# Turning the first half of x block by block in the prologue of a one-core fp32 decoder step

## The chip, the cores and the metric

The kernel runs on one core of one Trainium2 chip. The metric is the device time of one execution in microseconds; the time before is the median of three runs. The profile shows one execution. TensorE appears as two rows: PE (matmuls) and PEld (loads of the stationary operand); DVE is VectorE, ACT is ScalarE, POOL is GpSimd, SP is SyncE, which issues nearly all DMAs.

## What is computed

One layer of a hybrid decoder over 1024 new tokens and 8 x 8 decode tokens, width 1024: a half-step SwiGLU FFN (`ffn1`), token mixing (a pooling branch and a Mamba-2 SSD branch), a second half-step FFN, a final RMSNorm. The change touches only the start, which prepares and begins the first FFN:

```python
def rmsnorm(x, g):
    y = xf * lax.rsqrt(jnp.mean(xf * xf, axis=-1, keepdims=True) + EPS)
    return (y * g.astype(jnp.float32)).astype(x.dtype)

def swiglu(x, w_in, w_out):
    gu = x @ w_in
    g, u = gu[..., :D_FF], gu[..., D_FF:]
    return (jax.nn.silu(g) * u) @ w_out
...
x = x + 0.5 * swiglu(rmsnorm(x, norm_ffn1[l]), ffn1_w_in[l], ffn1_w_out[l])
```

## The kernel before, in words

Everything is fp32. A product is made of three fp32r products: each operand is split into a high part (`hi`, `wh`: the value rounded to fp32r) and a low part (`lo`, `wl`: the value minus its high part), and TensorE computes wh·hi, wh·lo and wl·hi (`products`, `mm` at L176). Tokens are handled in two halves: half 0 has 512 prompt tokens, half 1 has 512 prompt tokens and the 64 decode tokens.

`load_x(h, out)` prepares one half. It loads x in blocks of 128 tokens, each as two tiles `xin` of 128 x 512 (L905, on SyncE's queue). For each block ACT squares both tiles and sums along the row (L912) into the columns of `ss`. When all blocks of the half are squared, DVE adds the two sums and scales them (L915, L916), GpSimd raises to the power -0.5 (`rsqrt`, L378), and DVE multiplies the identity by each block's factor (L922), which gives diagonal matrices `dg`. TensorE then turns and normalizes x at once: for each of the eight 128-channel groups k, four matmuls of an `xin` block against its diagonal fill one PSUM bank `ptx` (tag "ps", of which there are 8 - N_PDF = 2 banks; the other six have tag "pd"). ACT copies the bank times the RMSNorm gain to `xn` (L935), DVE rounds the same bank to `hi` (L936), and DVE (even k) or GpSimd (odd k) subtracts to get `lo` (L941). ACT and DVE do not read one bank at the same time. For half 0 `hi` and `lo` lie side by side in one tile `hl`. Half 1 has a ninth group of small matmuls `pxs` for the decode tokens.

The order of work is written as generators ("chains"). A chain is due at a value of `pe[0]`, the kernel's own running count of TensorE time, to which `mm` adds the columns / 2400 us (four times that where the moving operand is not fp32r); `tick()` after each group of matmuls steps the chains that are due, and `finish` runs one to its end. The tile framework then orders each engine's instructions by this trace order, priorities and readiness in its own schedule, and puts in all waits. So an engine's queue is fixed before the run, and an instruction waits in it for the one ahead.

At the start, `load_x` for half 0 is stepped five times (loads, then the four blocks' squares), the first four weight tiles of ffn1 are loaded and split (`load_w`, L305 to L309, kept in `ahead`; ACT makes `wh` at L308, DVE `wl` at L309; three buffers each), and `load_x` for half 1 is stepped once; it continues X1_AT = 4.0 later. The loads that must not go first are held back by `hold`: a 1x1 copy by GpSimd (L283) into the tile from something that is known late, here half 0's `ss`. Then `ffn` calls `operands`: for each half it finishes `load_x`, starts `combine` as a chain due T_AT = 2.0 later, and runs the half's plain blocks: `ffn_in_plain` computes a 128-row block of the gate and up products in two "pd" banks `pg` and `pu`, three blocks for half 0 and two for half 1. `combine` makes the sums of x that the remaining blocks, which use a Winograd scheme (matmuls `pw`), need: GpSimd subtracts (`sub`, L521), ACT and DVE split the results into tiles `X` (`put`, L529 and L530).

Of the kernel before, what the change touches and what calls it, by code (L numbers as in the profile page):

```python
# [52 lines left out]
F_Y = 0.5  # L53
X1_AT = 4.0
T_AT, T_PACE = 2.0, 1.5
TURN_AT, CONST_AT = 60.0, 40.0
HP, HP_ST, HP_EV, HP_SC = 40, 0, 60, 80
SETS = (((0,), (1,), (2,), (3,)), ((0, 1), (2,), (3,)))
# [16 lines left out]
def tile_hybrid_pool_ssd_macaron(  # L75
# [45 lines left out]
    def fx(dt=F32, name="x"):  # L121
        if stage["name"] == "mix":
            return act((P, 576), dt, name)
        return stage["p"].tile([P, 592], dt, tag="fx", bufs=N_FX, name=nm(name))

    def psum(tag="ps", name="ps"):
        npd = stage["npd"]
        return stage["ps"].tile([P, 512], F32, tag=tag, bufs=npd if tag == "pd" else 8 - npd, name=nm(name))
# [18 lines left out]
    def start(gen, delay=0.0):  # L147
        c = Chain(gen, delay)
        chains.append(c)
        return c  # L150
# [24 lines left out]
    def mm(out, lhsT, rhs, start=True, stop=True, free=False):  # L175
        T.matmul(out, lhsT, rhs, start=start, stop=stop, skip_group_check=free)  # L176
        pe[0] += max(out.free_size(), 64) / 2400.0 * (1 if rhs.dtype == F32R else 4)
# [59 lines left out]
    Abc = cp.tile([P, NH], F32, tag="Abc", name="Abc")  # L237
    Dcol = cp.tile([P, 16], F32, tag="Dcol", name="Dcol")
    hp = [0]
    late = []  # L240

    def load_consts():

# [38 lines left out]

        G.tensor_copy(t[:1, :1], src)  # L283

    def load_w(w, k0, nk, c0, ncol=P, behind=None, keep=False):

        if (k0, c0) in ahead:
            return ahead.pop((k0, c0))
        if (w.tensor.name, k0, c0) in parted:
            nth[0] += 1  # L290
            out = []
            for t, src in zip(("wh", "wl"), parted[w.tensor.name, k0, c0]):
                if nth[0] % 2:
                    o = sp.tile([P, 4 * P], F32, tag="wraw", bufs=N_RAW, name=nm(t)).bitcast(F32R)
                else:
                    o = sp.tile([P, 4 * P], F32R, tag=t, bufs=N_W, name=nm(t))
                o = o[:, : nk * P]
                dma(o.bitcast(F32), src)
                out.append(o.rearrange("p (k c) -> p k c", c=ncol))
            return tuple(out)  # L300
        raw, wh, wl = (sp.tile([P, 4 * P], d, tag=t, bufs=n, name=nm(t))[:, : nk * ncol]
                       for t, d, n in (("wraw", F32, N_RAW), ("wh", F32R, N_W), ("wl", F32R, N_W)))
        if behind is not None:
            hold(raw, behind)
        dma(raw.rearrange("p (k c) -> p k c", c=ncol),  # L305
            w[k0 * P : (k0 + nk) * P, c0 : c0 + ncol].rearrange("(k p) c -> p k c", p=P))
        with tc.high_priority(hp[0]):
            S.activation(wh, raw, AF.Copy)  # L308
            V.tensor_tensor(wl, raw, wh.bitcast(F32), op=ALU.subtract)  # L309
        if keep:  # L310
            to = [dp.tile([P, nk * P], F32, tag=nm("part"), name=nm("part")) for _ in range(2)]
            for a, b in zip(to, (wh, wl)):
                dma(a, b.bitcast(F32))
            parted[w.tensor.name, k0, c0] = to
        return wh.rearrange("p (k c) -> p k c", c=ncol), wl.rearrange("p (k c) -> p k c", c=ncol)
# [190 lines left out]
                after(p, i, banks[i])  # L506
                tick()

    def combine(h, xn, hi, lo, hl, X, pace):

        n = NPAIR[h]
        f, s_ = slice(0, n), slice(n, 2 * n)
        for p, i0, cs in (("1", 0, f), ("2", 4, f), ("3", 4, s_)):
            X[p] = [(hi[i0 + i][:, cs], lo[i0 + i][:, cs]) if h else hl[i0 + i][:, :, cs] for i in range(4)]
        for p in "6574":
            X[p] = []

        def sub(out, a, b):  # L520
            G.tensor_tensor(out, a, b, op=ALU.subtract)  # L521

        def put(src, p, a=None, b=None):
            both = None
            if a is None:
                t = act((P, 576), F32R, "X")
                a, b = t[:, f], t[:, s_]
                both = t[:, : 2 * n].rearrange("p (a b) -> p a b", a=2)
            S.activation(a, src, AF.Copy)  # L529
            V.tensor_tensor(b, src, a.bitcast(F32), op=ALU.subtract)  # L530
            X[p].append((a, b) if h else both)

        for i in range(4):
            a, b = xn[i], xn[4 + i]
            sub(a[:, s_], a[:, s_], a[:, f])
            t2 = fx(name="t2")[:, f]
            sub(t2, b[:, s_], a[:, s_])
            put(t2, "6")
            put(a[:, s_], "5")
            yield pace  # L540
            sub(a[:, f], t2, a[:, f])
            sub(b[:, f], b[:, f], t2)
            put(a[:, f], "7")
            yield pace
        yield None
        for i in range(4):
            put(xn[4 + i][:, f], "4", hi[i][:, s_], lo[i][:, s_])
            if h == 0:
                X["4"][i] = hl[i][:, :, s_]
            yield pace  # L550
# [150 lines left out]
        yield SUM_PACE  # L701
        dma(*late_.pop(0))

    def operands(prep, plain):

        X, behind = [{}, {}], []
        for h in HALVES:
            finish(prep[h][0])
            x = prep[h][1][0]
            gen = combine(h, x[3], x[1], x[2], x[4], X[h], T_PACE)  # L710

            def first(gen):
                for p in gen:
                    if p is None:
                        return
                    yield p

            c = start(first(gen), T_AT)
            plain(x[:3])
            behind.append(start(rest(c, gen)))  # L720
        for c in behind:
            finish(c)
        return X

    def ffn(wi, wo, prep, after, half=None, side=None):

        def plain(x):
            for ff in range(N_PLAIN[x[0]]):  # L730
                ffn_in_plain(wi, ff, x)

        X = operands(prep, plain)
        if side:
            side = start(side, PART_AT)
        for ff in range(N_PLAIN[1], N_PLAIN[0]):
            ffn_in(wi, ff, [(1, X[1])])
        for ff in range(N_PLAIN[0], NFF - N_APART):
            ffn_in(wi, ff, [(h, X[h]) for h in HALVES])
        for h in HALVES:  # L740
            for ff in range(NFF - N_APART, NFF):
                ffn_in(wi, ff, [(h, X[h])])
        if side:
            finish(side)
        second(wo, after, half)
# [143 lines left out]
    def load_x(h, out):  # L889
# [16 lines left out]
                raws[-1].append(t)  # L906
        late.append(ss)
        yield X1_AT if h else 0.2
        for i, (_, c0, c) in enumerate(blocks):
            for q in range(2):  # L910
                junk = act((P, 512), name="junk")
                S.activation(junk[:c], raws[i][q][:c], AF.Square, accum_out=ss[:c, q, i : i + 1])  # L912
            yield 0.5
# [6 lines left out]
        dg = [dg[:, i * P : i * P + b[2]] for i, b in enumerate(blocks)]  # L920
        for i, (_, c0, c) in enumerate(blocks):
            V.tensor_scalar_mul(dg[i][:c, :c], ident[:c, :c], ss[:c, 2, i : i + 1])  # L922
        if h == 1:
            pq = psum("ps", "pxs")
            for k in range(KD):
                mm(pq[:, k * NS : (k + 1) * NS], raws[4][k // 4][:NS, (k % 4) * P : (k % 4 + 1) * P], dg[4][:NS, :NS])
        hi, lo, xn, hl = [None] * KD, [None] * KD, [None] * KD, [None] * KD
        for k in range(KD):
            pt = psum("ps", "ptx")
            for i in range(4):  # L930
                mm(pt[:, i * P : (i + 1) * P], raws[i][k // 4][:, (k % 4) * P : (k % 4 + 1) * P], dg[i])
            x = fx(name="xn") if k >= 4 else act((P, 576), name="xn")
            a, b, both = (act((P, 576), F32R, "hi"), act((P, 576), F32R, "lo"), None) if h else pair(576)
            g = cols[:, i_g1 + k : i_g1 + k + 1]
            S.activation(x[:, :512], pt, AF.Copy, scale=g)  # L935
            V.tensor_scalar_mul(a[:, :512], pt, g)  # L936
            if h == 1:
                ps_ = pq[:, k * NS : (k + 1) * NS]
                S.activation(x[:, 512:N], ps_, AF.Copy, scale=g)
                V.tensor_scalar_mul(a[:, 512:N], ps_, g)  # L940
            (G if k % 2 else V).tensor_tensor(b[:, :N], x[:, :N], a[:, :N].bitcast(F32), op=ALU.subtract)  # L941
            hi[k], lo[k], xn[k], hl[k] = a, b, x, both
            yield 0.9
        out.append((h, hi, lo, xn, hl))
# [410 lines left out]
    st = open_stage("ffn1", N_PDF)  # L1355
    finish(start(load_cols(0, nr0)))
    prep1 = [(start(load_x(h, o)), o) for h, o in ((0, []), (1, []))]
    for _ in range(5):
        prep1[0][0].step()
    for kb in (0, 4):  # L1360
        for c0 in (0, FF):
            ahead[kb, c0] = load_w(wi1, kb, 4, c0, behind=late[0][:1, 0, :1] if kb else None)
    prep1[1][0].step()

    def turn():
# [10 lines left out]
        yield from part(ffn2_w_in[0], [(kb, 4, c0 + ff * P) for ff in range(N_PLAIN[0]) for kb in (0, 4) for c0 in (0, FF)])  # L1376
        yield from part(w_o[0], [(kb, 4, m * P) for m in range(KD) for kb in (0, 4)])

    ffn(wi1, ffn1_w_out[0], prep1, after1, side=side())
    ahead_d = in_proj(prep1m)  # L1380
    st.close()

# [587 lines left out]
```

## Time and profile before

| | before |
|---|---|
| median of 3 runs | 2871.04 us (2869.55 to 2874.98) |
| the profiled execution | 2877.41 us, span 2875.6 us |
| mean granted TensorE clock | 0.989 |
| busy, share of the span | PE 97%, PEld 91%, DVE 65%, POOL 48%, ACT 47% |
| instructions | 54690 |

Times in the profile count from the start of the span. A line such as L912 is the kernel line that issued the instruction; all matmuls of the kernel have L176 and are told apart by the tile that they write. In a row of the timeline the first number is the start, the second the length, and the square brackets give how long the engine had been idle and what ended that. One matmul of full fp32 operands, such as `ptx`, shows as two instructions.

### The profile page before, as it was taken

To read this page: it belongs to the slowest core of one execution; us is meant where nothing else is said; L and a number is where in the kernel's file an instruction comes from. 1 tells how busy PE (TensorE), PEld (TensorE's weight loads), DVE (VectorE), ACT (ScalarE), POOL (GpSimd) and SP (SyncE) were. 2 spreads that over 40 slices of the span, in tenths; PEclk is the share of its full clock that TensorE was granted. 3 is DMA by queue.
4 is the path that set the end of the run, shared out by engine and by line. 5 is a ranking of instruction groups with operands and counts; after the bars stand their busy time and mean duration, and the time that the engine had idled before them with its cause. 6 is when DMAs were issued, how large, how long until landed. Compare 5 with 4: busy or idle time off the path is not lost.

```text
span 2875.6 us, 54690 instructions
## 1 busy us (share of the span) xinstructions
PE 2775.5 (97%) x19834; PEld 2606.6 (91%) x19834; DVE 1879.0 (65%) x2912; ACT 1364.5 (47%) x3024; POOL 1378.5 (48%) x1406
## 2 busy tenths in 40 slices
PE   7999999999999999999989999899999999999998
PEld 5999999899889999999988887678999999998997
DVE  6665565777884586867765767776665554457675
ACT  5444444643454565554554446556233434445433
POOL 6566566543442355554622332332235766664522
PEclk9999999999999999999999999999999999999999
DMA  4565554787745455544377788887775332337865
GB/s 132 180 209 193 175 161 151 248 295 250 238 130 161 154 167 168 180 155 137 100 234 231 213 251 268 261 272 216 235 242 176 107 99 94 99 114 257 286 202 183
DMA packets 533488, 548.02 MB, mean 191 GB/s; under 512 B 42836, under 2 KB 373704, under 8 KB 533208
## 3 DMA queue, kind: packets, MB, share of 16 engines
q1 hardware_dynamic: 533200, 544.51, 59.5%
q8 instruction: 156, 2.56, 0.4%
q14 instruction: 116, 0.95, 0.1%
q10 hardware_dynamic: 16, 0.00, 0.0%
HBM read 391.82 MB, written 152.78 MB: 189 GB/s over the span
## 4 chain that ended last, share of the span: by engine, by line
PE 75%; DMA 7%; DVE 6%; issue 4%; POOL 4%; ACT 2%; SPq 1%; POOLq 0%; ACTq 0%; DVEq 0%
PE pw L176 43%; PE po L176 10%; PE pso L176 5%; PE pg L176 3%; PE pbp L176 3%; PE pwo L176 3%; PE pu L176 2%; DMA hr<-xq 1%; PE pgm L176 1%; DMA hp<-xq 1%; PE pyd L176 1%; PE pst L176 1%; DVE hr L781 1%; DVE wl L459 1%; POOL s L676 1%
## 5 line engine op out<-in xcount | busy, mean ns | idle before, releaser
L176 PE MATMUL pw<-X,wh 128*128 128x288 f32 (+2 forms) x2832 | 627.5, 310 | 5.0 <-ACT t L604 2.7
L176 PEld LDWEIGHTS pw<-X,wh 128*128 128x128 f32 x2832 | 462.1, 189 | 27.3 <-ACT t L604 3.2
L176 PE MATMUL pw<-X,wl 128*128 128x288 f32 (+1 forms) x1644 | 473.6, 288 | 0.8 <-DVE wl L459 0.8
L459 DVE TENSOR_TENSOR wl<-s,wh 128x512 fp32r<-128x512 f32 x288 | 245.2, 853 | 247.1 <-ACT wh L458 232.4
L176 PE MATMUL pw<-hl,wh 128*128 128x256 f32 (+1 forms) x1536 | 391.7, 328 | 3.6 <-ACT t L580 2.3
L452 POOL TENSOR_TENSOR s<-wraw,wraw 128x512 f32<-128x512 f32 x144 | 198.9, 1381 | 332.8 <-DVE wl L459 210.3
L176 PE MATMUL pw<-hi,wh 128*128 128x288 f32 x1120 | 331.7, 296 | 2.6 <-DVE t L616 1.9
L176 PE MATMUL pw<-hi,wl 128*128 128x288 f32 x1120 | 329.8, 294 | 0.0
L176 PE MATMUL pw<-lo,wh 128*128 128x288 f32 x1120 | 329.6, 294 | 0.0
L176 PEld LDWEIGHTS pw<-X,wl 128*128 128x128 f32 x1644 | 311.7, 190 | 1.0 <-DVE wl L459 1.0
L176 PE MATMUL pw<-hl,wl 128*128 128x256 f32 x1072 | 300.6, 280 | 0.9 <-DVE wl L459 0.9
L176 PEld LDWEIGHTS pw<-hl,wh 128*128 128x128 f32 x1536 | 258.8, 189 | 24.9 <-ACT t L580 2.9
L759 POOL TENSOR_TENSOR ws<-wraw,wraw 128x512 f32<-128x512 f32 x120 | 179.8, 1507 | 200.9 <-DMA wraw<-in_ffn_w_out_dram 88.5
L459 DVE TENSOR_TENSOR wl<-wraw,wh 128x512 fp32r<-128x512 f32 x216 | 185.3, 858 | 124.2 <-ACT wh L458 118.9
L458 ACT ACTIVATE wh<-s 128x512 fp32r<-128x512 f32 x288 | 181.2, 630 | 136.2 <-PE pw L176 110.0
L176 PEld LDWEIGHTS pw<-hi,wh 128*128 128x128 f32 x1120 | 210.5, 188 | 9.5 <-DVE t L616 2.5
L176 PEld LDWEIGHTS pw<-lo,wh 128*128 128x128 f32 x1120 | 210.6, 188 | 0.0
L176 PEld LDWEIGHTS pw<-hi,wl 128*128 128x128 f32 x1120 | 210.1, 188 | 0.0
L458 ACT ACTIVATE wh<-wraw 128x512 fp32r<-128x512 f32 x216 | 135.8, 629 | 151.4 <-PE pw L176 130.7
L176 PEld LDWEIGHTS pw<-hl,wl 128*128 128x128 f32 x1072 | 202.9, 189 | 1.9 <-DVE wl L459 1.9
L176 PE MATMUL po<-hh,wh 128*128 128x272 f32 x848 | 179.9, 294 | 10.1 <-ACT wh L767 8.7
L176 PE MATMUL po<-hr,wh 128*128 128x272 f32 x848 | 178.1, 291 | 3.8 <-DVE hr L781 3.8
(403 smaller groups left out, 6773.3 us busy)
## 6 DMA issues: line engine op xcount, KB each, us to landing
wraw<-in_ffn_w_out_dram SPq DMA_DIRECT2D x240, 256.0 KB
wraw<-in_ffn_w_in_dram SPq DMA_DIRECT2D x188, 256.0 KB
wraw<-in_w_in_dram SPq DMA_DIRECT2D x144, 256.0 KB
wh<-part SPq DMA_DIRECT2D x116, 256.0 KB
wl<-part SPq DMA_DIRECT2D x116, 256.0 KB
hr<-xq SPq DMA_DIRECT2D x106, 272.0 KB
xq<-s SPq DMA_DIRECT2D x66, 272.0 KB
xq<-g SPq DMA_DIRECT2D x62, 272.0 KB
```

What stands on the lines that cost most here:

```text
L176: T.matmul(out, lhsT, rhs, start=start, stop=stop, skip_group_check=free)
L452: G.tensor_tensor(t, a, b, op=op)
L458: S.activation(wh, a, AF.Copy)
L459: V.tensor_tensor(wl, a, wh.bitcast(F32), op=ALU.subtract)
L676: G.tensor_tensor(out[:, a], x0[:, a], y[:, b0], op=op)
L759: G.tensor_tensor(s, raws[0], raws[1], op=ALU.subtract if p in MINUS2 else ALU.add)
L781: V.tensor_tensor(t[:, :n].bitcast(F32R), t[:, :n], a[:, :n].bitcast(F32), op=ALU.subtract)
```

## The change

Half 0 no longer waits for its last block. Eight PSUM banks (six of tag "pd", two of "ps") are taken for the eight groups at once. As each block's squares are done, its own factor is computed (add, scale, power, diagonal for one column), and its eight matmuls fill its quarter of all eight banks. When the fourth block is done, the banks are emptied by `leave_x`, which both halves share. In it, for half 0, the `hi` of odd groups is rounded by ACT instead of DVE, and all `lo` parts are made by DVE. Half 1 is turned as before, bank by bank.

The first weight tile is loaded and split ahead of the squares in the trace; the other three tiles' splits are pinned behind everything that was traced before on their engines, and the ACT copy and the DVE rounding of half 0's group 4 are pinned behind these splits. GpSimd's subtractions in `combine` for half 0 are queued behind a 1x1 copy that waits for the fourth `lo` part, and that chain falls due at T_AT1 = 9.0 instead of T_AT = 2.0. The second half's first step, the chain of constants and that of turning x again are started when `pe[0]` already holds half 0's transposes.

```diff
+T_AT1 = 9.0
...
         with tc.high_priority(hp[0]):
-            S.activation(wh, raw, AF.Copy)
-            V.tensor_tensor(wl, raw, wh.bitcast(F32), op=ALU.subtract)
+            pin(S.activation(wh, raw, AF.Copy))
+            pin(V.tensor_tensor(wl, raw, wh.bitcast(F32), op=ALU.subtract))
...
+        if gate is not None:
+            gate = G.tensor_copy(gate, lo[3][:1, :1].bitcast(F32)).ins
+
         def sub(out, a, b):
-            G.tensor_tensor(out, a, b, op=ALU.subtract)
+            if gate is None:
+                G.tensor_tensor(out, a, b, op=ALU.subtract)
+                return
+            with tc.issue_after(gate):
+                G.tensor_tensor(out, a, b, op=ALU.subtract)
...
-            c = start(first(gen), T_AT)
+            c = start(first(gen), T_AT if h or gate is None else T_AT1)
...
         yield X1_AT if h else 0.2
+        if h == 0:
+            pts = [psum("pd" if k < 6 else "ps", "ptx") for k in range(KD)]
+            for i in range(4):
+                cut = slice(i, i + 1)
+                for q in range(2):
+                    junk = act((P, 512), name="junk")
+                    S.activation(junk, raws[i][q], AF.Square, accum_out=ss[:, q, cut])
+                V.tensor_tensor(ss[:, 2, cut], ss[:, 0, cut], ss[:, 1, cut], op=ALU.add)
+                V.tensor_scalar(ss[:, 2, cut], ss[:, 2, cut], 1.0 / D, EPS, op0=ALU.mult, op1=ALU.add)
+                rsqrt(ss[:, 3, cut], ss[:, 2, cut])
+                dg = act((P, P), name="dg")
+                V.tensor_scalar_mul(dg, ident, ss[:, 3, cut])
+                for k in range(KD):
+                    mm(pts[k][:, i * P : (i + 1) * P], raws[i][k // 4][:, (k % 4) * P : (k % 4 + 1) * P], dg)
+                yield 0.5
+            yield from leave_x(h, out, pts, None)
+            return
...
+    def leave_x(h, out, pts, pq):
+        N = NTOK[h]
+        def pin_w4(ins):
+            for w in pinned:
+                if w.ins.engine == ins.ins.engine:
+                    tc.add_manual_dep(ins.ins, w.ins.name, mybir.DependencyInfo(
+                        mybir.DependencyClass.NoSync, mybir.DependencyReason.DATA), reason="keep_in_program_order")
+            return ins
...
         for k in range(KD):
+            pt = pts(k) if h else pts[k]
...
-            S.activation(x[:, :512], pt, AF.Copy, scale=g)
-            V.tensor_scalar_mul(a[:, :512], pt, g)
+            pin = (lambda i: i) if h or k != 4 else pin_w4
+            pin(S.activation(x[:, :512], pt, AF.Copy, scale=g))
+            if h == 0 and k % 2:
+                S.activation(a[:, :512], pt, AF.Copy, scale=g)
+            else:
+                pin(V.tensor_scalar_mul(a[:, :512], pt, g))
...
-            (G if k % 2 else V).tensor_tensor(b[:, :N], x[:, :N], a[:, :N].bitcast(F32), op=ALU.subtract)
+            (G if k % 2 and h else V).tensor_tensor(b[:, :N], x[:, :N], a[:, :N].bitcast(F32), op=ALU.subtract)
...
-    for _ in range(5):
+    prep1[0][0].step()
+    first_w = load_w(wi1, 0, 4, 0)
+    for _ in range(4):
         prep1[0][0].step()
+    ahead[0, 0] = first_w
     for kb in (0, 4):
-        for c0 in (0, FF):
-            ahead[kb, c0] = load_w(wi1, kb, 4, c0, behind=late[0][:1, 0, :1] if kb else None)
+        for c0 in (FF,) if kb == 0 else (0, FF):
+            ahead[kb, c0] = load_w(wi1, kb, 4, c0, behind=late[0][:1, 0, :1] if kb else None,
+                                pin=lambda i: pinned.append(tc.keep_in_program_order(i)))
     prep1[1][0].step()
...
-    ffn(wi1, ffn1_w_out[0], prep1, after1, side=side())
+    ffn(wi1, ffn1_w_out[0], prep1, after1, side=side(), gate=late[0][:1, 3, 4:5])
```

More of the change, by code (lines that the diff above doesn't have):

```diff
@@ L239, in tile_hybrid_pool_ssd_macaron @@
     hp = [0]
-    late = []
+    late, pinned = [], []
     def load_consts():
@@ L283, in hold, with load_w @@
         G.tensor_copy(t[:1, :1], src)
-    def load_w(w, k0, nk, c0, ncol=P, behind=None, keep=False):
+    def load_w(w, k0, nk, c0, ncol=P, behind=None, keep=False, pin=lambda i: i):
         if (k0, c0) in ahead:
@@ L507, in wino, with combine @@
                 tick()
-    def combine(h, xn, hi, lo, hl, X, pace):
+    def combine(h, xn, hi, lo, hl, X, pace, gate=None):
         n = NPAIR[h]
@@ L702, in sums, with operands @@
         dma(*late_.pop(0))
-    def operands(prep, plain):
+    def operands(prep, plain, gate=None):
         X, behind = [{}, {}], []
@@ L709, in operands @@
             x = prep[h][1][0]
-            gen = combine(h, x[3], x[1], x[2], x[4], X[h], T_PACE)
+            gen = combine(h, x[3], x[1], x[2], x[4], X[h], T_PACE, None if h else gate)
             def first(gen):
@@ L723, in operands, with ffn @@
         return X
-    def ffn(wi, wo, prep, after, half=None, side=None):
+    def ffn(wi, wo, prep, after, half=None, side=None, gate=None):
         def plain(x):
@@ L731, in plain @@
                 ffn_in_plain(wi, ff, x)
-        X = operands(prep, plain)
+        X = operands(prep, plain, gate)
         if side:
@@ L922, in load_x, with turned @@
             V.tensor_scalar_mul(dg[i][:c, :c], ident[:c, :c], ss[:c, 2, i : i + 1])
[L923 to L927, printed above, removed]
+        pq = psum("ps", "pxs")
         for k in range(KD):
+            mm(pq[:, k * NS : (k + 1) * NS], raws[4][k // 4][:NS, (k % 4) * P : (k % 4 + 1) * P], dg[4][:NS, :NS])
+        def turned(k):
             pt = psum("ps", "ptx")
@@ L931, in load_x @@
                 mm(pt[:, i * P : (i + 1) * P], raws[i][k // 4][:, (k % 4) * P : (k % 4 + 1) * P], dg[i])
+            return pt
+        yield from leave_x(h, out, turned, pq)
+    def leave_x(h, out, pts, pq):
[6 more added lines that the diff above has]
+            return ins
+        hi, lo, xn, hl = [None] * KD, [None] * KD, [None] * KD, [None] * KD
+        for k in range(KD):
+            pt = pts(k) if h else pts[k]
             x = fx(name="xn") if k >= 4 else act((P, 576), name="xn")
```

## The prediction

> **What bounds the kernel now.** I read the page first, then the busy time by stretch over the first 103 us, then the timeline and the chain of waits there, because the diff touches only what happens before ffn1's Winograd products (`pw`).
>
> ```profile
> PE 2775.5 (97%) x19834; PEld 2606.6 (91%) x19834; DVE 1879.0 (65%) x2912; ACT 1364.5 (47%) x3024; POOL 1378.5 (48%) x1406
> PE   7999999999999999999989999899999999999998
> PE 75%; DMA 7%; DVE 6%; issue 4%; POOL 4%; ACT 2%; SPq 1%; POOLq 0%; ACTq 0%; DVEq 0%
> ```
>
> TensorE is busy 97% of the span, and its first slice of 72 us is the emptiest one. TensorE's work is the same after the change, so only its idle time can be won or added. The stretches below give it (columns: stretch, length, then busy time and instruction count of PE, PEld, DVE, ACT, POOL; granted clock; DMA).
>
> ```profile
> 14.05:20.04 5.99, 5.52 (x25) 4.94 (x25) 3.85 (x8) 1.38 (x2) 0.56 (x1) 1.00 1.08 375
> 20.04:34.96 14.92, 14.53 (x84) 11.83 (x82) 11.56 (x15) 11.90 (x31) 13.54 (x15) 1.00 0.45 104
> 34.96:37.02 2.06, 0.01 (x1) 0.03 (x1) 1.15 (x6) 0.00 (x0) 2.06 (x8) 1.00 0.00 0
> 37.02:50.00 12.98, 12.98 (x81) 11.28 (x82) 9.25 (x17) 6.84 (x17) 5.98 (x12) 1.00 0.29 75
> 50.00:60.00 10.00, 8.75 (x50) 6.97 (x50) 8.51 (x14) 4.99 (x12) 8.55 (x8) 1.00 0.05 0
> 66.40:69.49 3.09, 1.00 (x5) 0.50 (x4) 3.09 (x5) 0.93 (x3) 3.09 (x4) 1.00 0.65 163
> 69.49:75.53 6.04, 6.04 (x20) 4.81 (x20) 4.03 (x5) 0.71 (x2) 5.88 (x7) 0.72 0.73 235
> 75.53:103.00 27.47, 27.33 (x204) 26.87 (x203) 17.01 (x31) 12.41 (x30) 7.34 (x6) 1.00 0.49 147
> ```
>
> The first 20 us are preparation; from 20.04 to 75.53 TensorE does half 0's three plain blocks `pg`/`pu` mixed with transposes; after 75.53 it is full. Inside it idles about 2.06 us at 35, 1.25 us between 50 and 60, and 2.09 us at 67, after which its clock is 0.72 for 6.04 us (6.04 x 0.28 = 1.7 us lost).
>
> The start in detail, from the timeline (start, length):
>
> ```profile
> 7.18 0.63 ACT L912 ACTIVATE junk<-xin 128x512 f32<-128x512 f32 x1 [1.93 <-DMA xin<-in_x_prompt_dram]
> 7.71 0.19 ACT L912 ACTIVATION_READ_ACCUMULATOR junk<-xin 128x1 f32 x1
> ...
> 11.81 0.19 ACT L912 ACTIVATION_READ_ACCUMULATOR junk<-xin 128x1 f32 x1
> ...
> 12.65 1.03 POOL L378 TENSOR_TENSOR xss<-xss,mhalf 128x4 f32<-128x4 f32 x1 [5.81 <-DVE xss L916]
> ...
> 13.71 0.29 DVE L922 TENSOR_SCALAR dg<-ident,xss 128x128 f32<-128x128 f32 x1 [1.25 <-POOL xss L378]
> 13.92 1.28 DVE L309 TENSOR_TENSOR wl<-wraw,wh 128x512 fp32r<-128x512 f32 x2
> ...
> 14.05 1.22 PE L176 MATMUL ptx<-dg,xin 128*128 128x128 f32 x4 [11.54 <-DVE dg L922]
> ...
> 15.46 2.93 PE L176 MATMUL ptx<-dg,xin 128*128 128x128 f32 x12 [0.18 <-DMA wraw<-in_ffn_w_in_dram]
> ...
> 18.67 1.61 PE L176 MATMUL ptx<-dg,xin 128*128 128x128 f32 x8 [0.28 <-DVE hl L936]
> ...
> 20.04 0.71 PE L176 MATMUL pg<-hl,wh 128*128 128x512 f32 x2
> ...
> 20.82 1.06 PE L176 MATMUL ptx<-dg,xin 128*128 128x128 f32 x8
> ```
>
> Block 0's two squares are done at 7.71 + 0.19 = 7.90, block 3's at 12.00; from there to the first transpose takes 2.05 us. All four blocks wait for the last. Each turned bank of half 0 is 8 instructions, 64 in all; 4 + 12 + 8 = 24 run before the first `pg` at 20.04, 40 after it.
>
> **The change part by part.**
>
> *Transposes per block.* Block 0 can start at 7.90 + 2.05 = 9.95 (a one-column power instead of a four-column one may shorten that; I take no gain). The first 16 instructions of before took (1.22 + 2.93) / 16 = 0.26 us each, the later ones 1.06 / 8 = 0.133. So 16 x 0.26 + 48 x 0.133 = 10.5 us, ending at 20.45; block 3's diagonal is there by about 14 and hides behind blocks 0 to 2, as do the added sums, powers and scalings per block. The first `pg` comes at 20.45 instead of 20.04: 0.4 us late. But 40 x 0.133 = 5.3 us of transposes are out of the way behind it. Net 4.9 us for TensorE. The slow first instructions are where the Trainium skill's "TensorE: Matmul & The Clock Gate", Part 1, puts a half clock until some 3.4 us of steady work; the durations agree, the granted-clock column (1.00) does not show it. By that rule alone the warm-up moves under the DMA wait and the sum is the same.
>
> *Weights.* The first load is traced earlier; its DMA already is SyncE's first, and behind the eight loads of x it would still be 10 us early, so nothing. The other splits are pinned behind the blocks, so the 1.28 us of `wl` that stood between the first diagonal and the others goes; with block 3 hidden that is worth nothing.
>
> *Leaving the banks.* The rows for the durations:
>
> ```profile
> 18.65 0.69 DVE L941 TENSOR_TENSOR hl<-xn,hl 128x512 fp32r<-128x512 f32 x1
> ...
> 21.53 0.74 POOL L521 TENSOR_TENSOR xn<-xn 128x256 f32<-128x256 f32 x1
> ...
> 21.82 0.99 DVE L941 TENSOR_TENSOR hl<-xn,hl 128x512 fp32r<-128x512 f32 x1
> ```
>
> ```profile
> L935 ACT ACTIVATE xn<-ptx,cols 128x512 f32<-128x512 f32 x15 | 10.3, 687 | 9.9 <-PE ptx L176 9.9
> ...
> L308 ACT ACTIVATE wh<-wraw 128x512 fp32r<-128x512 f32 x11 | 6.8, 629 | 7.6 <-PE pg L176 7.5
> ...
> L936 DVE TENSOR_SCALAR hl<-ptx,cols 128x512 fp32r<-128x512 f32 x8 | 6.0, 749 | 4.4 <-ACT xn L935 4.2
> ...
> L941 POOL TENSOR_TENSOR hl<-xn,hl 128x512 fp32r<-128x512 f32 x4 | 5.1, 1284 | 0.4 <-DVE hl L936 0.4
> ```
>
> GpSimd loses 4 x 1.28 = 5.1 us. DVE loses 4 roundings (4 x 0.75 = 3.0) and gains 4 lo parts (4 x 0.69 = 2.8): even. ACT gains 4 x 0.69 = 2.8 us. Per two banks DVE then needs 0.75 + 2 x 0.69 = 2.13 us, ACT 3 x 0.69 = 2.07, and TensorE takes 12 matmuls x 0.228 (0.68 / 3, row below) = 2.7. So the leaves stay ahead of TensorE, except at bank 4: its ACT copy and DVE rounding are pinned behind the split of the fourth weight tile, and there are three buffers, so that split waits until TensorE has used the first tile up, after bank 3. Then 0.63 (wh) + 0.69 (wl) + 0.75 (hi) + 0.69 (lo) = 2.8 us pass, of which the `pu` matmuls of bank 3 (0.7) and the first products of bank 4 hide part. Bounds: 0 (if ACT and DVE run it while TensorE still has bank 3) to 2.1; I take 1.0, the middle.
>
> *Sums held back.* A 1x1 copy on GpSimd waits for lo part 3; half 0's 20 sums queue behind it, and the second half's reciprocal root behind those. What waits for them are the rounded X, first needed by `pw`, far later:
>
> ```profile
> 102.58 9.52 PE pw L176 x72
> ```
>
> So the delay is free; the gain is that lo parts 0 to 3 run at 0.69 instead of 0.99. For lo parts 4 to 7 the trace prices a GpSimd neighbour at 0.30 each, 1.2 us on DVE, under the 0.3 us per bank that DVE is ahead. The Trainium skill's "SBUF — State Buffer", Who interferes with whom, speaks against the move: a DVE instruction with two SBUF inputs and a reading GpSimd one exclude each other for the whole instruction. By it each lo could wait a full 0.74 us sum, 3.0 us in all, 1.8 us more than by the row.
>
> *Second half.* Its chain:
>
> ```profile
> 33.16 0.68 PE pu L176 x3
> ...
> 34.97 2.05 issue
> ```
>
> ```profile
> 32.44 0.19 ACT L912 ACTIVATION_READ_ACCUMULATOR junk<-xin 64x1 f32 x1
> ...
> 34.62 1.21 POOL L378 TENSOR_TENSOR xss<-xss,mhalf 128x5 f32<-128x5 f32 x1 [0.17 <-DVE xss L916]
> ...
> 35.87 1.05 DVE L922 TENSOR_SCALAR dg<-ident,xss 128x128 f32<-128x128 f32 x5 [1.07 <-POOL xss L378]
> ```
>
> TensorE waited 2.05 us at 34.97 for these diagonals, last square 32.63 plus 4.4 us. The second half's chain falls due X1_AT = 4.0 us (in the kernel's own count of TensorE time) after its first step. Before, that step stood ahead of half 0's transposes (6.8 us of the count), so the chain was overdue when the matmuls began; now it stands behind them, and the squares are traced 4.0 us later among the matmuls: 4.0 / 0.2133 = 19 matmuls of 512 columns, or 4.3 us at 0.228. TensorE, ahead by 4.9 - 1.0 = 3.9, reaches the place at 34.97 - 3.9 + 4.3 = 35.4. The diagonals come at 37.02 plus 0 to 2.8 us (ACT's added load; 0 if its idle time takes it in). A wait of 1.6 to 4.4, I take 3.0: 0.9 more than before.
>
> *Sum.* -4.9 + 1.0 + 0.9 = -3.0 us. The profiled execution took 2877.41 us with a span of 2875.6; it is 6.4 above the median of 2871.04, so from the median: 2868.0.
>
> **The rivals.**
>
> *The late stall goes too.* These rows are the wait at 67:
>
> ```profile
> 34.40 0.41 DVE L530 TENSOR_TENSOR X<-xn,X 128x256 fp32r<-128x256 f32 x1
> ...
> 65.31 1.99 DVE L530 TENSOR_TENSOR X<-xn,X 128x256 fp32r<-128x256 f32 x2
> ...
> 68.16 2.49 DVE L309 TENSOR_TENSOR wl<-wraw,wh 128x512 fp32r<-128x512 f32 x2
> ...
> 69.49 0.50 PE L176 MATMUL pu<-hl,wl 128*128 128x512 f32 x1 [2.09 <-DVE wl L309]
> ```
>
> Two X of 0.41 took 1.99 beside GpSimd, and `wl` stood behind them. With TensorE and so the weight buffers some 3 us earlier, `wl` can come ahead of them. Then 2.09 + 1.7 of slow clock go, and 2.06 at 35 if the second half is early: 3.0 + 5.85 = 8.9 us, 2862. For it: the stall is an accident of order. Against it: DVE and GpSimd are full there (3.09 of 3.09 each).
>
> *Nothing is won, because the second half sets the pace.* From 37.02 on everything could hang on the second half's diagonals and on DVE (8.51 of 10 at 50 to 60). If they come when they did, TensorE's lead becomes waiting: 2871. Against it: TensorE is full from 37.02 to 50.
>
> *Slower: ACT is the new wait.* The second half's squares can queue behind half 0's twelve ACT copies. From 18.6: 12 x 0.69 + 3 wh x 0.63 + two or three X (1.2) + 10 squares at 0.69 spacing = 18.3, so 36.9, plus 4.4 = 41.3. That is 4.2 us later than 37.02, and a wait of over 5 us; if the clock falls after it as after 67, 1.7 us more: +5.9, 2877. It decides once the diagonals come after about 41. Against it: ACT idles before 18 with the second half's x already landing, 1.38 busy of 5.99.
>
> **How the numbers follow.** A measurement here tells about 0.2% (5.7 us) from no change. Forecast 2868: 0.35; second half paces, 2871: 0.12; late stall gone, 2862: 0.34; ACT slower, 2877: 0.13; the rest, 0.06 (0.04 faster, 0.02 slower), for changes of order later on. So faster 0.38, same 0.47, slower 0.15. The likeliest alone spans 2865 to 2871 (its two unknown costs at their ends, 0 and 2.1, -0.5 and 2.3); with both outer cases the range is 2858 to 2878.
>
> **What would show it.** Right: the first `ptx` at about 10, all 64 instructions done near 20.5, the first `pg` there, no `ptx` of half 0 after it; half 0's plain blocks ending 3 us before 75.53. A wait of about 1 us at bank 4 for DVE, and 1.6 to 4.4 us before `pxs`. Lo parts 0 to 3 at 0.69 us and the first L521 sum after the third of them. Wrong: `pxs` after 41, a low clock after it, or no wait at 67 at all.

## The result, and the profile after

| | before | after |
|---|---|---|
| median | 2870.3 us (2865.16 to 2874.98, 4 runs) | 2887.48 us (2884.0 to 2888.24, 4 runs) |
| profiled execution | 2877.41 us, span 2875.6 | 2887.84 us, span 2886.1 |
| mean granted clock | 0.989 | 0.990 |

The ratio is 1.0052, 95% interval 1.0041 to 1.0064: some 15 us slower (the medians differ by 17.2), where 3 us faster was forecast and the range ended at 2878. First the page of the changed kernel: busy time of each engine, and TensorE's 40 slices of 72 us.

```profile
PE 2776.5 (96%) x19834; PEld 2606.4 (90%) x19834; DVE 1872.1 (65%) x2918; ACT 1365.6 (47%) x3028; POOL 1367.9 (47%) x1406
PE   7899999999999999999998999899999999999998
```

TensorE's work is the same within 1.0 us, as forecast; idle time was added. The first slice is as empty as before, and the second fell from 9 to 8. The start, from the changed kernel's timeline (start, length, then the idle time and what ended it):

```profile
8.39 0.56 POOL L379 TENSOR_TENSOR xss<-xss,mhalf 128x1 f32<-128x1 f32 x1 [2.25 <-DVE xss L925]
9.33 9.31 PE L177 MATMUL ptx<-dg,xin 128*128 128x128 f32 x64 [6.59 <-DVE dg L928]
18.61 1.29 DVE L986 TENSOR_TENSOR hl<-xn,hl 128x512 fp32r<-128x512 f32 x2
...
18.64 0.49 PE L177 MATMUL pg<-hl,wh 128*128 128x512 f32 x1
...
21.96 0.17 POOL L522 COPY xss<-hl 1x1 f32<-1x1 f32 x1 [6.91 <-DVE hl L986]
22.10 2.81 POOL L529 TENSOR_TENSOR xn<-xn 128x256 f32<-128x256 f32 x4
...
26.18 0.50 PE L177 MATMUL pg<-hl,wh 128*128 128x512 f32 x1 [1.54 <-DVE hl L981]
...
38.86 1.03 DVE L947 TENSOR_SCALAR dg<-ident,xss 128x128 f32<-128x128 f32 x5 [1.35 <-POOL xss L379]
...
40.15 1.97 PE L177 MATMUL pxs<-dg,xin 64*128 64x64 f32 x16 [1.35 <-DVE dg L947]
```

All this is the change as described: 64 transposes in one stretch, the first `pg` at 18.64 (1.40 earlier than before's 20.04), lo parts at 0.65 us each while GpSimd is quiet, its sums from 22.10 on. The wait at bank 4 is 1.54 us, that for the second half's diagonals 1.35. If the same matmul is looked up in both traces (by its number among those that write `pg` and `pu`), the changed kernel leads by 9.4 us at 61 us of before's time. Not all of this is won: it has then done 32 of half 1's 64 `ptx` instructions, the kernel before all of them, and the other 32 take it some 3.5 us. At half 1's first matmul the same work lies behind both, and the lead there is 75.53 - 67.96 = 7.6 us. Before:

```profile
75.53 0.42 PE L176 MATMUL pg<-hi,wh 128*128 128x288 f32 x2
```

After, with the waits in which the lead is then lost:

```profile
67.96 0.42 PE L177 MATMUL pg<-hi,wh 128*128 128x288 f32 x2
...
69.80 0.54 PE L177 MATMUL pu<-hi,wh 128*128 128x288 f32 x2 [0.88 <-ACT wh L309]
...
74.85 0.85 PE L177 MATMUL pu<-hi,wl 128*128 128x288 f32 x2 [4.12 <-DVE wl L310]
```

These are half 1's first plain products. By 83 us 0.7 of the lead is left, and at 102, where `pw` starts, the changed kernel is 0.9 late; at 139 it is 4.7 late, at 253 9.9, at 337 14.7, and from there to 1230 about 16. (The two profiled spans end 10.5 us apart, because the profiled execution of the kernel before, 6.4 us above its median, loses 5.5 behind 1230.) So there are two questions: where the lead of 7.6 us goes, and where 15 us are lost in code that the diff does not touch. What TensorE waited for from 100 to 400 us (total, times, longest), before and then after:

```profile
PE pw L176 <- DVE t L616: 1.9, 2, 1.3
PE pw L176 <- ACT t L614: 0.7, 1, 0.7
```

```profile
PE pw L177 <- DVE t L624: 6.0, 2, 3.5
PE pw L177 <- ACT t L622: 3.2, 2, 2.9
PE pw L177 <- DVE t L590: 0.7, 1, 0.7
```

The waits are 9.9 us in place of 2.6. The other half is TensorE's clock behind them: it was granted 0.91 over 130 to 150 us, 0.89 over 240 to 270 and 0.94 over 330 to 360, where the kernel before has 1.00 in all three. An estimate from these is 20 x 0.09 + 30 x 0.11 + 30 x 0.06 = 6.9 us; with the 7.3 us of waits that is the loss between 102 and 337, 13.8, within 0.4.

One of these losses, followed back. After, and at the end what SyncE's stores `xq` waited for from 120 to 136 us:

```profile
111.82 0.50 SPq L997 DMA_DIRECT2D xin<-in_x_prompt_dram  x1
...
113.19 2.02 SPq L479 DMA_DIRECT2D wraw<-in_ffn_w_in_dram  x2
...
118.33 1.28 POOL L453 TENSOR_TENSOR s<-wraw,wraw 128x512 f32<-128x512 f32 x1 [2.89 <-DMA wraw<-in_ffn_w_in_dram]
...
128.97 0.38 SPq L324 DMA_DIRECT2D pr<-in_ffn_w_in_dram  x1
...
133.31 0.63 ACT L371 ACTIVATE ph<-pr 128x512 fp32r<-128x512 f32 x1 [4.71 <-DMA pr<-in_ffn_w_in_dram]
...
134.80 0.40 PE L177 MATMUL pw<-hi,wh 128*128 128x288 f32 x1 [2.92 <-ACT t L622]
...
SPq L690 <- POOL s L685: 10.5, 3, 7.6
```

The same rows before:

```profile
111.96 1.83 SPq L478 DMA_DIRECT2D wraw<-in_ffn_w_in_dram  x2
...
115.05 0.42 SPq L952 DMA_DIRECT2D xin<-in_x_prompt_dram  x1
...
115.61 1.30 POOL L452 TENSOR_TENSOR s<-wraw,wraw 128x512 f32<-128x512 f32 x1 [1.54 <-DVE wl L459]
...
125.74 0.45 SPq L323 DMA_DIRECT2D pr<-in_ffn_w_in_dram  x1
...
131.72 0.40 PE L176 MATMUL pw<-hi,wh 128*128 128x288 f32 x1 [0.73 <-ACT t L614]
...
SPq L682 <- POOL s L677: 6.9, 2, 6.0
```

`xin` belongs to `turn_x`, the chain that turns x again. Its load stands ahead of the Winograd weights `wraw` on SyncE's queue now, not behind; GpSimd's sum waits 2.89 us for them, SyncE's later stores wait for GpSimd's sums, and `pr`, the load of a side chain (`part`) behind them, is issued 3.2 us later. ACT, in order, waits for `pr` with `t`, which TensorE needs, behind it.

### The profile page after: what moved, and what is told of

The parts are those of the page before. It is cut to its first block, busy times and chain, and to the rows that moved or that the text cites. A ratio compares the mean times of both kernels' runs of the same rounds, so it can differ in the third digit from the quotient of the medians.

```text
span 2886.1 us, 54704 instructions
## 1 busy us (share of the span) xinstructions
PE 2776.5 (96%) x19834; PEld 2606.4 (90%) x19834; DVE 1872.1 (65%) x2918; ACT 1365.6 (47%) x3028; POOL 1367.9 (47%) x1406
## 4 chain that ended last, share of the span: by engine, by line
PE 74%; DMA 8%; DVE 6%; POOL 4%; issue 3%; ACT 3%; SPq 1%; POOLq 0%; ACTq 0%; DVEq 0%
PE pw L177 44%; PE po L177 8%; PE pso L177 5%; PE pg L177 3%; PE pbp L177 3%; PE pwo L177 2%; PE pu L177 2%; DMA wraw<-in_ffn_w_out_dram 1%; DMA hp<-xq 1%; DMA hr<-xq 1%; PE pgm L177 1%; DMA wraw<-in_ffn_w_in_dram 1%; PE pyd L177 1%; PE pst L177 1%; POOL s L684 1%
## 5 line engine op out<-in xcount | busy, mean ns | idle before, releaser
L767 POOL TENSOR_TENSOR ws<-wraw,wraw 128x512 f32<-128x512 f32 x120 | 173.4, 1452 | 210.7 <-DMA wraw<-in_ffn_w_out_dram 85.8
L460 DVE TENSOR_TENSOR wl<-wraw,wh 128x512 fp32r<-128x512 f32 x216 | 178.2, 825 | 127.8 <-ACT wh L459 124.0
L177 PE MATMUL po<-hh,wl 128*128 128x272 f32 x848 | 177.9, 291 | 4.3 <-DVE wl L776 3.8
```

The costliest lines, as they stand in the source:

```text
L460: V.tensor_tensor(wl, a, wh.bitcast(F32), op=ALU.subtract)
L767: G.tensor_tensor(s, raws[0], raws[1], op=ALU.subtract if p in MINUS2 else ALU.add)
```

## The experiments

Two theories for the 15 us: (1) the turning chain starts later in the order, because `start(turn(), TURN_AT)` now stands behind half 0's 64 transposes, 6.8267 us of `pe[0]`, and its load meets other work; or (2) it follows from the new prologue itself. For the lead lost at 70 to 75 (the expectations below call it 9 us, by the matmul at 60 us; in e1 it is 7.4 at half 1's first matmul): (A) weights issued too late by SyncE, or (B) `wh` and `wl` standing behind other work in ACT's and DVE's queues.

**e1: the changed kernel, both due times rebased.**

```diff
-TURN_AT, CONST_AT = 60.0, 40.0
+TURN_AT, CONST_AT = 60.0 - 6.8267, 40.0 - 6.8267
```

> The changed kernel with TURN_AT and CONST_AT taken back by 6.83 (53.17 and 33.17), so that the chains that turn x again and load the constants fall due as many us after half 0's plain blocks begin as they did before. Theory 1 (the loss is made after 100 us, because the turning chain, now started behind half 0's transposes in the count, is late and its instructions stand among the Winograd blocks in another order): the three waits of 2.9, 3.5 and 2.6 us at 135, 253 and 346 us shrink to what the kernel before shows at these matmuls (0.7, 1.3 and under 0.6), and the time falls by 10 to 17 us, to 2870 to 2877 and 0.998 to 1.002 of before. Theory 2 (the loss is made in the first 100 us, in leaving the banks and the second half's start): no fall, 2884 to 2890. Theory 3 (the early TensorE collides later with the sums, whatever the chain does): less than half of the loss goes.

Measured: 2869.99 us, ratio to before 0.9998 (0.999 to 1.0007). All 17.5 us are gone, with the whole new prologue in place. `xin` goes out at 114.61 us, behind the three `wraw` from 109.82 on, and `pr` at 125.39. TensorE's waits from 100 to 400 us are those of before:

```profile
PE pw L177 <- DVE t L624: 1.3, 1, 1.3
PE pw L177 <- ACT t L622: 0.8, 1, 0.8
```

**e2: the kernel before, its turning chain 6.8267 later.**

```diff
-TURN_AT, CONST_AT = 60.0, 40.0
+TURN_AT, CONST_AT = 60.0 + 6.8267, 40.0
```

> The kernel before, with TURN_AT alone raised by 6.83 to 66.83: nothing of the block-by-block turning. Theory 1: slower by 10 to 17 us, 2880 to 2887, with the same three long waits. Theories 2 and 3: within 4 us of before.

Measured: 2883.08 us, ratio 1.0046 (1.0031 to 1.006): 12.9 us slower, from one number, with the old prologue. `xin` goes out at 112.14, ahead of two `wraw` at 113.50, and `pr` at 129.41; the kernel is late by 5.1 us at 139, 10.8 at 253 and 13.3 at 337, and the long waits are at the same four places as in the changed kernel:

```profile
PE pw L176 <- DVE t L616: 3.7, 2, 2.0
PE pw L176 <- ACT t L614: 3.7, 2, 3.2
PE pw L176 <- DVE t L582: 2.0, 1, 2.0
```

Theory 1 is shown from both sides: one number takes the loss away and one brings it. That the path is the one through SyncE's queue is read from the traces, at one of the four places. Only this one shift was tried, so the runs don't say what other due times would cost.

**e12: the changed kernel, the turning chain alone rebased** (`TURN_AT = 60.0 - 6.8267`, `CONST_AT = 40.0`).

> The changed kernel with TURN_AT alone 6.8267 lower; the chain of constants stays 6.8 us of count later, as in the changed kernel. The rebased kernel moved both and came to 2870.0; delaying the turning chain alone in the kernel before cost 12.9 us, 4.6 less than the 17.5 between the changed and the rebased kernel. Theory 1 (the turning chain alone carries the loss): 2870, within 2, with no wait over 1.5 us for DVE or ACT at 131, 245 and 346. Theory 2 (the constants' later place carries the missing 4.6): 2874 to 2876, with the loss before 105 us.

Measured: 2874.62 us, ratio 1.0013 (1.0003 to 1.0022), 12.9 below the changed kernel and 4.6 above e1. The turning chain carries 12.9 of the 17.5 us, the same as in e2; the constants' chain carries the rest, as its theory 2 said. At 102 this kernel is 2.8 behind the kernel before, e1 0.5 ahead. Of these 3.3 us, 1.2 are there at 40 us already: without a longer wait, the clock of this execution was 0.57 over 28 to 32 us, that of e1 1.00. The other 2.0 are two waits for `wl` at 86 and 99 us, which the changed kernel has too (1.7 us in all) and e1 has not. The rest of the 4.6, and which instruction of that chain costs it, stays open.

**e3: e1 without the gate, half 0's sums due at T_AT = 2.0.**

```diff
-            gen = combine(h, x[3], x[1], x[2], x[4], X[h], T_PACE, None if h else gate)
+            gen = combine(h, x[3], x[1], x[2], x[4], X[h], T_PACE, None)
...
-            c = start(first(gen), T_AT if h or gate is None else T_AT1)
+            c = start(first(gen), T_AT)
```

> As e1, but GpSimd's subtractions of half 0 are not held behind the fourth lo part and their chain falls due at 2.0 as before. Each lo part of banks 0 to 3 would then run beside a subtraction: 0.30 us more each by the row of before, 1.2 us on DVE. If the holding back matters for the lead, the first plain block ends 1 to 2 us later than in e1 and the time is 0 to 2 us above e1; if it costs later (the sums crowd DVE at 60 to 80 us), e3 is 1 to 4 us below e1.

Measured: 2874.17 us, ratio 1.001 (1.0 to 1.002): 4 us above e1, more than the 0 to 2 expected. TensorE loses its lead early, at a weight that stands behind half 1's squares and half 0's rounded X on ACT's queue, and in this execution the clock behind it was 0.50 over 40 to 48 us; at half 1's first matmul it is 0.8 us behind the kernel before:

```profile
37.02 0.73 PE L177 MATMUL pg<-hl,wh 128*128 128x512 f32 x2 [2.38 <-ACT wh L309]
```

**e6: e1 with half 0's old split** (odd `hi` by DVE, odd `lo` by GpSimd).

```diff
-            if h == 0 and k % 2:
+            if False:
                 S.activation(a[:, :512], pt, AF.Copy, scale=g)
             else:
...
-            (G if k % 2 and h else V).tensor_tensor(b[:, :N], x[:, :N], a[:, :N].bitcast(F32), op=ALU.subtract)
+            (G if k % 2 else V).tensor_tensor(b[:, :N], x[:, :N], a[:, :N].bitcast(F32), op=ALU.subtract)
```

> e1 with half 0's odd banks emptied as before: hi rounded by DVE, lo subtracted by GpSimd (so ACT copies 8 instead of 12, and GpSimd has 4 x 1.28 us more). If ACT's added 2.8 us delay the second half's diagonals, pxs starts 1 to 3 us earlier than in e1 (40.4) and the time is 0 to 2 us lower; if the lo parts on GpSimd delay the first plain block, its end comes 1 to 3 us later and the time is 0 to 3 us higher.

Measured: 2875.18 us, ratio 1.0022 (1.0011 to 1.0034): about 5 us above e1, more than either expectation. At bank 4 TensorE waits 4.01 us for `hl`, 1.53 in e1:

```profile
24.88 3.45 DVE L310 TENSOR_TENSOR wl<-wraw,wh 128x512 fp32r<-128x512 f32 x1 [3.30 <-ACT wh L309]
...
29.05 0.50 PE L177 MATMUL pg<-hl,wh 128*128 128x512 f32 x1 [4.01 <-DVE hl L981]
```

The `wl` ahead of it on DVE took 3.45 us where 0.89 are seen in e1. Beside it run GpSimd's sums of half 0, 0.70 us each without a gap from 22.93 to 27.78, not its lo parts, which stand before and behind. In e1 the sums pause for 0.35 us at 25.1, while `wl` runs. So the old division lost by where the sums fell beside one weight; what the division is worth otherwise these two runs don't tell.

**e7: e1 without the pins** on the weights' splits and on group 4.

```diff
-                                pin=lambda i: pinned.append(tc.keep_in_program_order(i)))
+                                pin=lambda i: i)
```

> e1 without the pins: the weight splits and bank 4 are free to be ordered by the framework. My prediction priced the pin at bank 4 at 1.0 us of waiting (1.5 us were seen at 26 us). If the pin is what costs it, the wait at 26 us goes and the time is up to 2 us below e1. If the pin protects the fourth weight split, the wait there grows to 2 to 4 us and the time is 1 to 3 us above e1.

Measured: 2872.88 us, ratio 1.0008 (0.9995 to 1.0021). The wait of 1.53 us at bank 4 goes, for one of 1.32 at 28 us, and the time is 3 us above e1, so neither expectation fits whole. At half 1's first matmul it leads the kernel before by 7.8 us, e1 by 7.4; at 102 it is 2.0 late, behind waits of 1.25 us at 71 and 4.64 for `wl` at 81. What a prologue wins before half 1 does not count unless half 1 can use it.

**e4 and e5: the two loads of `Dcol` issued by ACT,** in e1 and in the kernel before.

```diff
-            dma(Dcol[hh * HD : (hh + 1) * HD, :], dsk[hh].partition_broadcast(HD))
+            nc.scalar.dma_start(Dcol[hh * HD : (hh + 1) * HD, :], dsk[hh].partition_broadcast(HD))
```

> e1 with one more edit: the two loads of Dcol (2 x 64 x 16 elements of 4 bytes) go out on ACT's DMA queue instead of SyncE's. Question: where did e1's lead of 9.2 us at 60 us go? In e1 the queue of SyncE is held from 47.7 to 65.5 us behind these loads, and the weights of half 1's second row block are issued at 68.8 us after a wait for Dcol; TensorE then waits 4.1 us at 75. Theory A (that queue eats the lead): the weights are issued by 62, the wait at 75 shrinks under 1.5 us, and the time falls 3 to 8 us below e1, to 2862 to 2867. Theory B (DVE eats it: the wl split stands behind seven X parts there, slowed by GpSimd): the weights come earlier but the wait stays over 3 us, and the time is within 2 us of e1.

> The kernel before with the Dcol loads on ACT's DMA queue; the order of all other instructions is the same. Theory A: here too the wait of 2.1 us at 69.5 and the low clock behind it go, since a weight load of that time took 5.7 us to issue: 2 to 4 us faster, 2866 to 2868. Theory B: no change beyond 1.5 us.

Measured: 2890.63 us, ratio 1.0072 (1.0052 to 1.0092), and 2881.21 us, ratio 1.004 (1.0025 to 1.0055). Both theories missed: the loads were taken off SyncE's queue, but not off the DMA engines. They ran 4 to 9 us earlier, ahead of everything that SyncE issued behind. ACT waited for a constant, and TensorE waited behind ACT (15.68 us at 69.57 in e4); here e4:

```profile
46.75 7.79 SPq L251 DMA_DIRECT2D tri<-in_tri_dram  x1
54.63 5.98 SPq L251 DMA_DIRECT2D strict<-in_strict_dram  x1
...
68.77 0.23 ACT L260 ACTIVATE Abc<-Abc 128x32 f32<-128x32 f32 x1 [17.36 <-DMA Abc<-in_a_log_dram]
```

So the two runs do not tell A from B; the load itself had to go.

**e8 and e9: `Dcol` loaded as rows of 128 bytes,** in e1 and in the kernel before.

```diff
-    Dcol = cp.tile([P, 16], F32, tag="Dcol", name="Dcol")
+    Dcol = cp.tile([P, 32], F32, tag="Dcol", name="Dcol")
...
-            dma(Dcol[hh * HD : (hh + 1) * HD, :], dsk[hh].partition_broadcast(HD))
+            dma(Dcol[hh * HD : (hh + 1) * HD, :], d_skip[0].partition_broadcast(HD))
...
+        pairs = Dcol.rearrange("p (q h) -> p q h", h=2)
+        V.tensor_copy(pairs[HD:, :, 0], pairs[HD:, :, 1])
```

The multiplication by `Dcol` in the SSD branch then reads every second column.

> The changed kernel with its turning chain rebased (2870.0 us), and Dcol loaded as whole rows of 32 elements (128 packets of 128 bytes in place of 2048 of 4 bytes), one small DVE copy for its upper half of partitions. In the rebased kernel the three bsel loads behind Dcol took 10.5 us to issue on SyncE (47.74 to 58.23) and no weights were issued between 42 and 58; at 75.06 PE waited 4.11 us for DVE's wl. Theory A (the lead of 9 us at 60 is lost because the second half's weights are issued late behind Dcol): the bsel loads issue in under 2 us, weights are issued from 50, the waits at 70 and 75 shrink from 5.0 to under 1.5 us, and the time falls to 2866 or below. Theory B (it is lost because ACT's and DVE's queues hold half 0's last X roundings ahead of wh and wl, slowed by GpSimd's sums, and DVE is 9 tenths busy from 50 to 80): weights land early, but the wait at 75 stays above 3 us and the time stays at 2870, within 2.

> The kernel before with the same load of Dcol as rows. There SyncE needed 10.5 us for the three bsel loads (48.19 to 58.72), and at 69.49 PE waited 2.09 us for DVE's wl. Theory A: the wait at 69 goes, and the time falls by about 2 us, to 2868. Theory B: DVE is 9.9 tenths busy from 60 to 70, the wait stays, and the time is the same within 1 us.

Measured: 2873.99 us, ratio 1.0011 (1.0002 to 1.0021), and 2872.17 us, ratio 1.0011 (1.0002 to 1.002). The three loads behind `Dcol` now issue within 2 us, and in e8 weights from 52 us on (58 in e1), but TensorE's waits are those of e1 (4.11) and, in e9, 2.12 us at 70 where the kernel before had 2.09. DVE is full up to the wait (e8):

```profile
71.02 1.26 DVE L539 TENSOR_TENSOR X<-xn,X 128x256 fp32r<-128x256 f32 x1
72.20 1.01 DVE L539 TENSOR_TENSOR X<-t,X 128x256 fp32r<-128x256 f32 x1
73.14 1.94 DVE L539 TENSOR_TENSOR X<-xn,X 128x256 fp32r<-128x256 f32 x2
75.00 1.27 DVE L311 TENSOR_TENSOR wl<-wraw,wh 128x512 fp32r<-128x512 f32 x1
...
76.33 0.85 PE L177 MATMUL pu<-hi,wl 128*128 128x288 f32 x2 [4.11 <-DVE wl L311]
```

Theory A falls, B stands: four X of half 0, 4.2 us beside GpSimd's sums, stand ahead of `wl`. In both kernels, clearing the clogged queue gained nothing. e8 is 4 us above e1. In the profiled executions 2.7 of these are there at 102, and the clock covers them: 0.60 against 1.00 over 28 to 32 us, and 0.60 against 0.86 over 76 to 84. Whether the new load costs anything stays open.

**e10: e1 with half 0's sums due earlier** (`T_AT1 = 5.0` in place of 9.0); **e11: e10 with e8's rows.**

> The rebased kernel with half 0's sums begun 5 us of count after its plain blocks begin in place of 9 (T_AT1); the gate at GpSimd stays. DVE is 0.49 and 0.56 busy from 30 to 50 and 0.99, 0.89 and 0.91 from 50 to 80. Theory B: some 4 us of X roundings move from the busy stretch to the idle one, the wait of 4.11 at 75 shrinks by 2 to 4 us, and the time falls to 2866 to 2868. Theory A: the order of the roundings is not what paces; the wait at 75 stays within 1 us and the time at 2870. A third way, seen without the gate: the roundings stand ahead of wh at 37, PE waits there over 2 us, and the time is 2872 or more.

> Both edits: Dcol as rows and half 0's sums begun at 5. If the two causes add (weights late and roundings late), the waits at 70 and 75 go together and the time is 2862 to 2865, the 9 us of lead at 60 being kept; if only one of them paces, the time is that of the better of the two single edits, within 1.5 us; if the roundings at 37 are in the way, it is above 2870.

Measured: e10 2868.8 us, ratio 0.9987 (0.9975 to 0.9999); e11 2867.61 us, ratio 0.9991 (0.9982 to 1.0). These are the two lowest medians, 2 to 3 us below the kernel before; at 0.1% and intervals that end at 0.9999 and 1.0, that is hardly told from none. The stretch from 70 to 80 (busy time of PE, PEld, DVE, ACT, POOL; clock; DMA) of e1, then of e10, and TensorE's wait in e10:

```profile
70.00:80.00 10.00, 5.87 (x31) 5.64 (x32) 9.12 (x10) 1.74 (x4) 9.92 (x11) 0.83 0.58 192
```

```profile
70.00:80.00 10.00, 8.40 (x50) 8.16 (x51) 6.71 (x9) 3.29 (x9) 9.92 (x11) 0.83 0.59 187
```

```profile
72.27 0.54 PE L177 MATMUL pu<-hi,wl 128*128 128x288 f32 x2 [1.60 <-DVE wl L310]
```

One X is left ahead of `wl`, DVE falls from 9.12 to 6.71 of 10, TensorE's wait from 4.11 to 1.60 us. That the X on DVE are what TensorE waits for is shown; what this is worth in the whole time, 1.2 us by the medians, is within the spread. e10 is 2.5 us ahead of the kernel before at 102, e1 0.5: of the 7.1 us that e10 leads by at half 1's first matmul, a third arrives. The 2862 to 2865 of causes that add did not come true.

## Why the prediction was wrong, step by step

*The failed step.* The prediction read the shift of `pe[0]` for one chain, X1_AT ("now it stands behind them"), and priced it at +0.9. The same shift moves the chains started by TURN_AT and CONST_AT, and for these its part by part held no term at all; what was left of them was "the rest, 0.06 ... for changes of order later on". They measured 12.9 and 4.6 us, 17.5 together, against 3.0 us of forecast gain. The chain of `turn_x` runs beside a stretch where TensorE was full, which the prediction took for safe; but its loads share SyncE's queue with the weights.

*Transposes per block*: right in kind, 0.5 too small. First `ptx` 9.33 (9.95 forecast), of which 0.47 is the one-column power, 0.56 us where 1.03 had been kept. The 64 took 9.31 us (10.5): 0.133 each counts the end of every group of eight, but the next instruction starts 0.81 us after such a group (44.88 to 45.69 in the changed kernel), 0.101 each. So the first `pg` came at 18.64 (20.45 forecast), 1.4 earlier than before; the 40 behind it are by this worth 4.0 us, not 5.3, and the two 5.4 against the 4.9 of the sum.

*Leaving the banks*: 1.54 us at bank 4 (1.0 taken, 0 to 2.1). Lo parts 0 to 3 took 0.65 us each (0.69 forecast); the later pairs took 2.27 and 2.31 us beside GpSimd (from 26.16 and 29.13), 0.50 more each than alone: 2.0 us, between the 1.2 by the row and the 3.0 by the rule of the Trainium skill that the prediction named. Bank 4 was not all: 0.43 and 0.18 us of waiting at banks 5 and 6 had no term.

*Second half*: 1.35 us (3.0 taken, 1.6 to 4.4): under the bounds. `pxs` ran at 40.15, 3.1 us later than before's 37.02 (0 to 2.8 taken), but TensorE came to the place at 38.8, not 35.4: 73 of half 0's matmuls stand ahead of `pxs`, 41 before, so 32 more where 19 were taken. The rival in which ACT is the new wait needed 41 and did not come. Its price was wrong too: 4.2 us more for `pxs` is not 4.2 us lost, since more matmuls run ahead of it. By the prediction's own sum a wait of 5.9 us is 3.9 more than before's, and with the slow clock -4.9 + 1.0 + 3.9 + 1.7 = 1.7 us, 2873 and not 2877.

*Sum*: half 0's plain blocks end 7.6 us earlier, not 3. The rival "the late stall goes too" came true at its place: the wait of 2.09 us in half 0's third block is gone, and the slow clock of 1.7 behind it. That leaves 3.8 for the prologue itself, near the 3.0 of the sum, but by luck in part, since its terms were off in both directions. Then all of it counted for nothing, which is the outcome of the rival "the second half sets the pace", given 0.12: e1 shows it at 2870, against 2871. Its reason was right by half. DVE does set the pace, through `wl`; the second half's diagonals cost 1.35 us. What was held against it ("TensorE is full from 37.02 to 50") is a stretch that ends before the place. A stall longer than the late one came instead, 0.88 and 4.12 us at half 1's first weights, and TensorE's clock behind it was again low (0.68 granted of 75 to 80):

```profile
75.00:80.00 5.00, 5.00 (x27) 5.00 (x28) 5.00 (x7) 1.22 (x3) 4.92 (x6) 0.68 0.36 125
```

*Sums held back, "so the delay is free"*: wrong as well. X itself is first needed by `pw`, but its roundings are queued on DVE ahead of what half 1 needs; e10 against e1 shows 2.5 us of wait from it. Without the hold (e3), they stand ahead of half 0's own weights instead. The rule of the Trainium skill that spoke against the move ("SBUF — State Buffer", Who interferes with whom) is that a DVE instruction with two SBUF inputs and a reading GpSimd one exclude each other. It fits here: an X of 0.41 us takes 0.97 to 1.26 beside sums of 0.95, at most nine tenths of a sum more. The prediction applied it to the lo parts alone.

## What to carry to other kernels

Where work is ordered by due times in a running count, moving any step across the point at which a chain is started moves that chain: list every chain that starts behind the step, and either rebase its due time or price each queue it lands in, long after the edit. A lead in the prologue is worth only what the next stage's slowest engine lets through; look for the busiest engine of that stage, not for TensorE's own idle time. When a lead is read from one matmul in two traces, see first that the same work lies behind it in both. Before a clogged queue is cleared, see whether the wait that matters has a full engine in front of it.

## What the runs showed of the hardware

Two loads of 1024 four-byte elements each, 8 KB in all, held up a queue far longer than their bytes: the three loads of 0.5 KB behind them took 10.5 us to issue (e1), and under 2 when `Dcol` came in 128 rows of 128 bytes (e8). Issued from another queue, they delayed SyncE's loads all the same (7.79 us to issue one of 64 KB in e4). GpSimd's power took 0.56 us for one column, 1.03 for four and 1.21 for five.

TensorE's granted clock fell after short waits, but not each time. The kernel before and e2 both waited 2.05 us ahead of `pxs`; over 40 to 44 us the clock was then 1.00 in the one and 0.50 in the other. After 1.54 us at bank 4 it was 1.00 over 28 to 32 us in the changed kernel, 0.57 in e12 and 0.60 in e8. That is some 1.7 us in 4 (4 x 0.43), so a difference of one or two microseconds between two profiled executions need not come from the kernels.
